# Norm products issued later, key normalisation moved to the last projection pairs, the gate's loops exchanged, and a second bank for the filler, in a hybrid attention and state-space block

## The chip, the cores and the metric

The kernel runs on one core of one Trainium2 chip. The metric is the time of one execution of the program on the device, in microseconds; a comparison goes by the median of several runs. A core has one matrix engine (PE, whose weight loads are listed apart as PEld), three engines for elementwise work (DVE, ACT and POOL), and an engine, SP, that in this kernel issues all the DMA transfers between the main memory and the on-chip buffers (SBUF). Matrix products land in PSUM, which is divided into banks of 128 x 512 single-precision numbers.

## The reference

One decoder layer in single precision, sequence 1024, width 2048. In one row per operation:

```
h = rms_norm(x) * gain
q, k, v, z_att, u, z_ssm, g_att, g_ssm = split(h @ w_in)            # widths 6 x 1024, 2 x 2048
q, k = rms_norm over each group of 64 channels, with gains           # 8 heads x 2 halves
w  = softmax(q0 k0^T / 8, causal) - lam * softmax(q1 k1^T / 8, causal)
y_att = rms_norm(w @ v, per head) * (1 - lam_init) * silu(z_att)
y  = gelu(diagonal state-space scan of u + d * u)
y_ssm = y * sigmoid(y @ w_glu + b_glu) * silu(z_ssm)
m  = sigmoid(g_att) * (y_att @ w_proj_att) + sigmoid(g_ssm) * (y_ssm @ w_proj_ssm)
out = x + m @ w_out
```

## The kernel before

Every large product keeps single-precision accuracy by splitting both operands into a high and a low part (`split`, lines 90 and 91: ACT rounds to the high part, DVE or POOL subtracts for the low one), and by three matrix products, high by high, high by low, low by high. A matrix instruction here multiplies a 128 x 128 block of weights by 128 x 512 activations. Everything is kept channels-first (128 channels on the partitions, 512 tokens along the row); a value called t is one of the two halves of the 1024 tokens.

The program has these stages in the order of time:

- **Projections.** The products with `w_in` are computed by a scheme of the Strassen-Winograd kind: a *pair* of output tiles (256 channels by 1024 tokens) over half of the 2048 input channels costs 7 block products of 12 matrix instructions (`products`, line 492), and additions on the results in place of an eighth product (`pair`). The first half of the input channels goes through `part`, which stores its results to `d_p`; the second half goes through `whole`, which loads them again (tag `q`, pool `qp`, line 555) and adds them (lines 571 to 582). Between is the state-space scan, whose result y lies in main memory as `d_yg`. The pairs of `whole` come in the order q (4 pairs, i = 0 to 3), k (4 to 7), v (8 to 11), z_att ("za", 12 to 15), z_ssm ("zs", 16 to 19), g_att ("ga", 20 to 27) and g_ssm ("gs", 28 to 35). The last two products of a pair (`rest`) are put off into the next pair by `pending` and `finish`.
- Each finished tile of `whole` goes through a function of its kind. `evac_q` and `evac_k` store it and call `norms`: ACT squares the tile, it is split (tiles `sh_`, two buffers, and `sl_`, one buffer, the same tags in which q, k and v are split for their stores), and two matrix products with a selector (line 975, into the banks `nps`) add up the squares of each group of 64 channels. `qk_norms` turns the 32 rows of sums into inverse roots; its three steps are called behind pairs n = 8, 10 and 12, that is, in the v pairs and the first za pair. `norms_k` has 16 tiles of k to normalise: load from `d_k` (line 1004, tag `ks`, one buffer), load the factors (`rb`, line 1007), multiply on DVE (line 1015), split, store. One step is called behind each pair from i = 12 on; the last ones where they fall. `evac_gate` computes silu(z) for za and zs (sigmoid on ACT, line 1034, product on POOL, line 1035) and the sigmoid for ga and gs (line 1037), and stores.
- **Gate** (`w_glu`): for each token half t and each of 8 column tiles ct, 24 matrix instructions (line 1135), the weights loaded (line 1121) and split anew for either half; y (line 1127) and silu(z_ssm) (line 1129) are loaded and multiplied on POOL (line 1130), times the sigmoid of the product on DVE (line 1138), split, stored to `d_ys` (line 1142).
- **Attention**, 8 heads of 8 query tiles, in the order `ORDER`. The matrix engine's order is written by hand here: scores (line 1178), mask (line 1181), DVE scales and takes the row's bound (line 1185), ACT exponentiates (line 1187), later PE transposes (line 1203) and multiplies by v (line 1215, bank `op`) and sums squares (line 1232, same bank). Between them *filler* instructions are fed, of which `FILL` gives the number behind each query tile: the products y_ssm @ `w_proj_ssm` (`ps_tile`, line 288). Each filler tile is 24 instructions into one bank (`ac2`), which DVE then multiplies by the gate g_ssm (line 292).
- **Tail**: what is left of the filler, the products with `w_proj_att`, and the products with `w_out` (line 1356).

Outside the attention the order on each engine is made by a list scheduler that simulates the program. The order is fixed in the program: each engine works its list in turn and waits at semaphores. SP's transfers are in one such list too.

Of the kernel before, what the change touches and what calls it, by code (L numbers as in the profile page):

```python
# [10 lines left out]
F32 = mybir.dt.float32  # L11
# [24 lines left out]
FILL = (10, 9, 10, 9, 10, 9, 10, 9)  # L36
# [31 lines left out]
def hybrid_block(ctx: ExitStack, tc: tile.TileContext, x_t, x_n, w_t, w_v, w_glu, w_pa, w_ps,  # L68
# [257 lines left out]
    with ExitStack() as pa_ctx:  # L326
# [158 lines left out]

        def products(ps, i, a, w, start):
            hs, ls = a
# [7 lines left out]
        pending = []  # L495
# [6 lines left out]
        def pair(w, a, out11, out21, out22, out12):  # L502
# [19 lines left out]
            u3 = post.tile([P, 512], F32, name="u3", tag="u3")  # L522
# [422 lines left out]
        qp = ev_ctx.enter_context(tc.tile_pool(name="qp", bufs=8, side="right"))  # L945
# [7 lines left out]
        def qk_norms():  # L953

            for t in range(2):
                v = stg.tile([32, 512], F32, name="nv", tag="sq")
                y = stg.tile([32, 512], F32, name="ny", tag="ny", bufs=1)
# [10 lines left out]
        def norms(src, row, t):  # L968

            sq = stg.tile([P, 512], F32, name="sq", tag="sq")  # L970
            A.activation(sq, src, AF.Square)
            hi, lo = split_tiles()
            split(hi, lo, sq)
            for n, m in enumerate((hi, lo)):
                T.matmul(nps[t], lhsT=sel[:, 32 - row:160 - row], rhs=m,
                         start=(n_norms[t] == 0), stop=(n_norms[t] == 31), skip_group_check=True)
                n_norms[t] += 1
# [63 lines left out]
        evacs = {"q": evac_q, "k": evac_k, "v": evac_v, "za": evac_gate(d_za, True), "zs": evac_gate(d_zs, True),  # L1041
                 "ga": evac_gate(d_ga, False), "gs": evac_gate(d_gs, False)}
        first = {kind: i for kind, i, _ in KINDS}
        for i, (kind, n) in enumerate(order):
# [3 lines left out]
            if n == 8:  # L1048
                steps = qk_norms()
            if n in (8, 10, 12):  # L1050
                next(steps, None)
            if i == 12:
                ks = norms_k()
            if i >= 12:
                next(ks, None)
        finish()
        ev_ctx.close()
# [39 lines left out]
        gl = gl_ctx.enter_context(tc.tile_pool(name="gl", bufs=3))  # L1097
# [7 lines left out]
        def yg_inputs(t):  # L1105
            def ld(k, hi, lo):
                r = wp.tile([P, 512], F32, name="ya", tag="value", bufs=2)
                D.dma_start(r, d_yg[k, :, t * 512:(t + 1) * 512])
                split(hi, lo, r)
            return ld  # L1110

        for t in range(2):
            tk = slice(t * 512, (t + 1) * 512)
            ya = act_half(act, yg_inputs(t))
            for ct in range(8):
                for _ in range(2 if 8 * t + ct > 2 else 0):
                    next(head0, None)
                ws = []
                for b in range(2):
                    raw = wp.tile([P, 4, P], F32, name="w_raw", tag="w_raw", bufs=5)  # L1120
                    D.dma_start(raw, w_glu[ct, :, 4 * b:4 * b + 4])
                    m = (2 * ct + b) % 7
                    hi, lo = (wp.tile([P, 4, P], F32R, name=n, tag=f"{n}{m}") for n in ("w_hi", "w_lo"))
                    split(hi, lo, raw)
                    ws.append((hi, lo))
                r = gl.tile([P, 512], F32, name="r", tag="r")
                D.dma_start(r, d_yg[ct, :, tk])
                z = gl.tile([P, 512], F32, name="z", tag="z")
                D.dma_start(z, d_zs[ct, :, tk])
                Q.tensor_tensor(r, r, z, ALU.mult)  # L1130
                ps = acc.tile([P, 512], F32, name="pg", tag="acc")
                for k in range(8):
                    wh, wl = (x[:, k % 4] for x in ws[k // 4])
                    for n, (x, y) in enumerate(((wh, ya[0][k]), (wh, ya[1][k]), (wl, ya[0][k]))):
                        T.matmul(ps, lhsT=x, rhs=y, start=(k == 0 and n == 0), stop=(k == 7 and n == 2))
                sg = gl.tile([P, 512], F32, name="sg", tag="sg", bufs=2)
# [303 lines left out]
```

## Time and profile before

| what | value |
|---|---|
| time before, median of 3 runs (lowest, highest) | 2805.34 us (2804.27, 2805.68) |
| the profiled execution's own time | 2804.28 us |
| its span in the profile | 2802.5 us |
| PE busy | 2695.5 us, 96%, 12402 matrix instructions |
| DVE, ACT, POOL busy | 66%, 43%, 27% |
| DMA moved | 487.82 MB, mean 174 GB/s |

A row of the profile names an engine, an operation with its output and its inputs, a line of the kernel, and times; "<-" behind an idle time names what ended it. A window gives, between two times from the span's start, the busy time of each engine with the number of its instructions in brackets, then the clock granted to PE as a share of full speed (PEclk), the share of the time in which the DMA engines were busy, and GB/s. A row of the waits gives an engine and line, what it waited for, the microseconds in total, how often, and the longest one. In a timeline, the columns are the start, the duration, the engine and line, the operation, and in square brackets the idle time of that engine before it. SPq, ACTq and the like are the engines' own sequences of issued transfers and semaphore waits.

### The profile page before, as it was taken

The page shows a single profiled execution, that of the slowest core. Times are in us where ns is not written, and L with a number is a line of the kernel's source. Part 1 is how long each engine was busy: PE and PEld are TensorE (multiplying, and loading weights), DVE is VectorE, ACT ScalarE, POOL GpSimd, SP SyncE. Part 2 cuts the span into 40 slices and gives each one's busy share as a digit, 9 for nine tenths or more (in the row PEclk, how much of TensorE's full clock was granted, in tenths as well). Part 3 has the DMA queues.
Part 4 walks back from the last instruction along what each step waited for, and adds up shares of the span by engine and source line. Part 5 has one row for each costly group of instructions (what it writes and reads, how often), then busy time and mean ns, then how long its engine had stood idle before and what let it go on. Part 6 is the DMA issues. An engine that isn't in the chain of part 4 may idle for free. (4 is left out here: it accounts for less than half of the span.)

```text
span 2802.5 us, 37947 instructions
## 1 busy us (share of the span) xinstructions
PE 2695.5 (96%) x12402; PEld 2205.5 (79%) x12402; DVE 1844.1 (66%) x3512; ACT 1205.9 (43%) x2359; POOL 743.7 (27%) x1101
## 2 busy tenths in 40 slices
PE   9999999999999998998899999789999999999999
PEld 8888788887878876776678888667878778888887
DVE  4998877777787776787676666457666575325432
ACT  6433455545455544433444444345555433223221
POOL 0002866565674011224442222212222200000000
PEclk9999999999999999999999999999999999999999
DMA  9653333333333454457765555976777386455453
GB/s 350 220 180 115 103 113 117 115 116 120 121 101 117 166 181 165 149 174 230 243 214 167 168 162 169 317 234 194 198 238 206 128 296 194 131 155 177 150 158 113
DMA packets 261926, 487.82 MB, mean 174 GB/s; under 512 B 33912, under 2 KB 44480, under 8 KB 261728
## 3 DMA queue, kind: packets, MB, share of 16 engines
q1 hardware_dynamic: 261728, 485.40, 53.7%
q8 instruction: 98, 1.61, 0.2%
q14 instruction: 100, 0.82, 0.1%
HBM read 345.72 MB, written 139.56 MB: 173 GB/s over the span
## 5 line engine op out<-in xcount | busy, mean ns | idle before, releaser
L492 PE MATMUL acc<-ah,w_hi 128*128 128x512 f32 x2128 | 841.6, 396 | 28.1 <-ACT u L523 22.8
L492 PE MATMUL acc<-ah,w_lo 128*128 128x512 f32 x2128 | 841.0, 396 | 0.0
L492 PE MATMUL acc<-al,w_hi 128*128 128x512 f32 x2128 | 840.2, 395 | 0.0
L90 ACT ACTIVATE w_hi<-w_raw 128x512 fp32r<-128x512 f32 x532 | 333.9, 629 | 523.3 <-PE o L1356 219.7
L91 DVE TENSOR_TENSOR w_lo<-w_raw,w_hi 128x512 fp32r<-128x512 f32 x474 | 338.4, 715 | 308.9 <-ACT w_hi L90 296.3
L492 PEld LDWEIGHTS acc<-ah,w_hi 128*128 128x128 f32 x2128 | 402.7, 189 | 120.6 <-ACT u L523 27.6
L492 PEld LDWEIGHTS acc<-ah,w_lo 128*128 128x128 f32 x2128 | 402.5, 189 | 87.7 <-issue 5.4
L492 PEld LDWEIGHTS acc<-al,w_hi 128*128 128x128 f32 x2128 | 402.9, 189 | 83.4 <-issue 2.0
L90 ACT ACTIVATE w_hi<-value 128x512 fp32r<-128x512 f32 x304 | 191.7, 630 | 313.3 <-DVE value L346 161.4
L91 DVE TENSOR_TENSOR w_lo<-value,w_hi 128x512 fp32r<-128x512 f32 x304 | 219.5, 722 | 61.3 <-ACT w_hi L90 53.7
L1356 PE MATMUL o<-w_lo,mh 128*128 128x512 f32 x512 | 199.2, 389 | 0.0
L1356 PE MATMUL o<-w_hi,ml 128*128 128x512 f32 x512 | 199.2, 389 | 0.0
L1356 PE MATMUL o<-w_hi,mh 128*128 128x512 f32 x512 | 195.3, 389 | 0.0
L581 POOL TENSOR_TENSOR u<-u,q 128x512 f32<-128x512 f32 x72 | 99.8, 1387 | 230.2 <-ACT u L514 120.7
L346 DVE TENSOR_TENSOR value<-w_raw 128x512 f32<-128x512 f32 x152 | 150.3, 989 | 2.7
L1185 DVE TENSOR_SCALAR_CACHE_REDUCE pe<-s,nrq 128x128 f32<-128x128 f32 (+7 forms) x128 | 100.1, 813 | 70.9 <-PE s L1181 58.9
L91 POOL TENSOR_TENSOR w_lo<-w_raw,w_hi 128x512 fp32r<-128x512 f32 x58 | 84.0, 1448 | 234.3 <-ACT w_hi L90 204.0
L575 POOL TENSOR_TENSOR p<-p,q 128x512 f32<-128x512 f32 x36 | 60.5, 1680 | 322.5 <-DVE acc L520 210.0
L288 PE MATMUL pc<-ah,w_hi 128*128 128x512 f32 x256 | 107.6, 420 | 25.4 <-DVE z L292 16.8
L1187 ACT ACTIVATE pe<-pe,mx 128x128 f32<-128x128 f32 (+7 forms) x128 | 98.5, 773 | 42.2 <-DVE pe L1185 42.0
L1356 PEld LDWEIGHTS o<-w_lo,mh 128*128 128x128 f32 x512 | 96.1, 188 | 20.0
L1356 PEld LDWEIGHTS o<-w_hi,mh 128*128 128x128 f32 x512 | 96.1, 188 | 19.9
(681 smaller groups left out, 4588.5 us busy)
## 6 DMA issues: line engine op xcount, KB each, us to landing
w_raw<-in_w_t_dram SPq DMA_DIRECT2D x288, 256.0 KB
q<-d_p SPq DMA_DIRECT2D x160, 256.0 KB
w_raw<-in_w_out_dram SPq DMA_DIRECT2D x128, 256.0 KB
d_p<-u SPq DMA_DIRECT2D x72, 256.0 KB
w_raw<-in_w_ps_dram SPq DMA_DIRECT2D x64, 256.0 KB
w_raw<-in_w_pa_dram SPq DMA_DIRECT2D x64, 256.0 KB
d_p<-ps SPq DMA_DIRECT2D x52, 256.0 KB
d_p<-p SPq DMA_DIRECT2D x36, 256.0 KB
```

What stands on the lines that cost most here:

```text
L90: A.activation(hi, src, AF.Copy)
L91: (eng or V).tensor_tensor(lo, src, hi.bitcast(F32), ALU.subtract)
L288: T.matmul(ps, lhsT=w[:, k % 4], rhs=b[k], start=(k == 0 and n == 0), stop=(k == 7 and n == 2))
L346: V.tensor_tensor(t, x, y, ALU.add)
L492: T.matmul(ps, lhsT=x[:, c], rhs=y[i][j], start=(start and j == 0 and n == 0), stop=(j == 3 and n == 2), skip_group_check=True)
L575: e.tensor_tensor(u, u, other(1), ALU.add)
L581: e.tensor_tensor(u, u, other(i), ALU.subtract)
L1185: V.tensor_scalar(pc[c][:, 0:w], sc[c][:, 0:w], nrq[:, 2 * h + c, tt:tt + 1], None, ALU.mult, ALU.min, accum_out=mx[:, c:c + 1])
L1187: ins = A.activation(pc[c][:, 0:w], pc[c][:, 0:w], AF.Exp, bias=mx[:, c:c + 1], scale=-1.0, accum_out=su[:, c:c + 1])
L1356: T.matmul(ps[i], lhsT=a[k][:, tt], rhs=w[:, 0], start=(k == 0 and n == 0), stop=(k == KT - 1 and n == 2))
```

## The change

1. `norms`: the two selector products are put on a list and issued when three more block products have begun (`postponed`, `tick`), and its split has tiles of its own (`nh`, `nl`, two buffers each). To make room, `qp` has 5 buffers in place of 8.
2. The PSUM copy `u3` of a pair alternates between two tiles in the pairs of `whole`.
3. The three steps of `qk_norms` come one pair later, and `norms_k` starts at i = 20 (the first ga pair) in place of i = 12 (the first za pair).
4. The zs tiles are multiplied by y as well as by the sigmoid: each of the 16 tiles loads y from `d_yg` (tag `ks`, one buffer) and has a DVE product more. The gate no longer loads y for this, and has no product on POOL.
5. The gate has the column tile in the outer loop, the token half in the inner one: each weight block is loaded and split once. Both halves of y are therefore held at once, the second in tiles of `kq`. The first column tile's weights and the first half of y are issued ahead of the last products of the projections.
6. In the attention the pool `wtp` is opened before `pex`, so the tiles of the exponentials lie elsewhere in SBUF.
7. The filler alternates between its bank and the bank `op` of the values, where no values or sums of squares are due; `give_bank` finishes a filler tile that holds `op` before these come. `FILL` feeds 74 instructions a head in place of 76.

```diff
-FILL = (10, 9, 10, 9, 10, 9, 10, 9)
+FILL = (10, 9, 9, 9, 10, 9, 9, 9)
...
+        tick, postponed = [0], []
+
         def products(ps, i, a, w, start):
+            tick[0] += 1
+            while postponed and postponed[0][0] <= tick[0]:
+                postponed.pop(0)[1]()
...
-            u3 = post.tile([P, 512], F32, name="u3", tag="u3")
+            turn[0] ^= 1
+            if more and turn[0]:
+                u3 = more[0].tile([P, 512], F32, name="u3", tag="u3", bufs=1)
+            else:
+                u3 = post.tile([P, 512], F32, name="u3", tag="u3")
...
-        qp = ev_ctx.enter_context(tc.tile_pool(name="qp", bufs=8, side="right"))
+        more.append(stg)
+        qp = ev_ctx.enter_context(tc.tile_pool(name="qp", bufs=5, side="right"))
...
-            hi, lo = split_tiles()
+            hi, lo = (stg.tile([P, 512], F32R, name=n, tag=n) for n in ("nh", "nl"))
             split(hi, lo, sq)
-            for n, m in enumerate((hi, lo)):
-                T.matmul(nps[t], lhsT=sel[:, 32 - row:160 - row], rhs=m,
...
+            def add():
+                for m in (hi, lo):
+                    T.matmul(nps[t], lhsT=sel[:, 32 - row:160 - row], rhs=m,
...
+            postponed.append((tick[0] + 3, add))
...
-        def evac_gate(dst, silu):
+        def evac_gate(dst, silu, src=None):
...
+                    if src is not None:
+                        y = stg.tile([P, 512], F32, name="y", tag="ks", bufs=1)
+                        D.dma_start(y, src[i, :, t * 512:(t + 1) * 512])
+                        V.tensor_tensor(st, st, y, ALU.mult)
                     Q.tensor_tensor(st, st, sg, ALU.mult)
...
-            if n == 8:
+            if n == 9:
                 steps = qk_norms()
-            if n in (8, 10, 12):
+            if n in (9, 11, 13):
                 next(steps, None)
-            if i == 12:
+            if i == 20:
                 ks = norms_k()
-            if i >= 12:
+            if i >= 20:
                 next(ks, None)
...
+        ahead = gate_weights(0)
+        ya = act_half(act, yg_inputs(0, lambda: wp.tile([P, 512], F32, name="ya", tag="value", bufs=2)))
         finish()
+        run(ks)
...
-        for t in range(2):
-            tk = slice(t * 512, (t + 1) * 512)
-            ya = act_half(act, yg_inputs(t))
-            for ct in range(8):
-                for _ in range(2 if 8 * t + ct > 2 else 0):
+        for ct in range(8):
+            ws, ahead = ahead, gate_weights(ct + 1) if ct < 7 else None
+            for t in range(2):
+                tk = slice(t * 512, (t + 1) * 512)
+                if 2 * ct + t > 1:
                     next(head0, None)
...
-                r = gl.tile([P, 512], F32, name="r", tag="r")
-                D.dma_start(r, d_yg[ct, :, tk])
-                z = gl.tile([P, 512], F32, name="z", tag="z")
-                D.dma_start(z, d_zs[ct, :, tk])
-                Q.tensor_tensor(r, r, z, ALU.mult)
+                r = gl.tile([P, 512], F32, name="r", tag="r", bufs=3)
+                D.dma_start(r, d_zs[ct, :, tk])
...
+        wtp = at.enter_context(tc.tile_pool(name="wtp", bufs=1))
         pex = at.enter_context(tc.tile_pool(name="pex", bufs=2))
-        wtp = at.enter_context(tc.tile_pool(name="wtp", bufs=1))
...
+        def filler_bank():
+            turn[0] ^= 1
+            if ended:
+                return bank(ssp, "s")() if turn[0] else bank(ac2)()
+            own[0] = bool(turn[0]) and (at_step[0] < NT - 2 or not 0.2 < at_step[0] % NT < 4.3)
+            return bank(tps, "op")() if own[0] else bank(ac2)()
...
+        def give_bank():
+
+            while own[0]:
+                owed[0] -= 1
+                step()
```

Three places show how the instructions move. The first is PE in the q pairs, where `acc<-` rows are block products and `nps` rows the selector products of the norms. Before:

```order
L975 MATMUL nps_11009<-sl__11252,sel 128x512
L975 MATMUL nps_11009<-sh__11278,sel 128x512
L975 MATMUL nps_11009<-sl__11279,sel 128x512
L975 MATMUL nps_11010<-sh__11322,sel 128x512
L492 MATMUL acc<-ah,w_hi 128x512
L492 MATMUL acc<-al,w_hi 128x512
```

and after:

```order
L497 MATMUL acc<-ah,w_lo 128x512
L987 MATMUL nps_11009<-nl,sel 128x512
L497 MATMUL acc<-ah,w_hi 128x512
L497 MATMUL acc<-al,w_hi 128x512
L497 MATMUL acc<-ah,w_lo 128x512
L497 MATMUL acc<-ah,w_hi 128x512
L987 MATMUL nps_11009<-nh,sel 128x512
L497 MATMUL acc<-al,w_hi 128x512
```

Four selector products stood in a row, each on another tile; now each stands alone among block products.

The second place is DVE in the projections: the product of k with its factors (L1015, then L1028), the product with y (L1051), and the additions that empty the banks (L571, L582, L520; then L580, L591, L525). Before, in the za pairs:

```order
L1015 TENSOR_TENSOR ks<-ks,rb 128x512
L91 TENSOR_TENSOR w_lo<-w_raw,w_hi 128x512
L366 TENSOR_TENSOR value<-value,w_raw 128x512
L571 TENSOR_TENSOR q<-acc,q 128x512
L91 TENSOR_TENSOR sl__15302<-ks,sh__15301 128x512
```

After, in the zs pairs and then in the ga pairs:

```order
L1051 TENSOR_TENSOR p_14095<-p_14095,y 128x512
L591 TENSOR_TENSOR u_14110<-acc,u_14110 128x512
L91 TENSOR_TENSOR w_lo<-value,w_hi 128x512
L91 TENSOR_TENSOR w_lo<-w_raw,w_hi 128x512
L366 TENSOR_TENSOR value<-value,w_raw 128x512
L1051 TENSOR_TENSOR u_14110<-u_14110,y 128x512
L580 TENSOR_TENSOR q<-acc,q 128x512
L91 TENSOR_TENSOR w_lo<-w_raw,w_hi 128x512
L1051 TENSOR_TENSOR q<-q,y 128x512
...
L591 TENSOR_TENSOR u_15246<-acc,u_15246 128x512
L1028 TENSOR_TENSOR ks<-ks,rb 128x512
L91 TENSOR_TENSOR w_lo<-w_raw,w_hi 128x512
L91 TENSOR_TENSOR sl__16114<-ks,sh__16113 128x512
L585 TENSOR_TENSOR p_15156<-acc,p_15156 128x512
L91 TENSOR_TENSOR w_lo<-value,w_hi 128x512
L346 TENSOR_TENSOR value<-value,w_raw 128x512
L1028 TENSOR_TENSOR ks<-ks,rb 128x512
```

The normalisation of k has gone from the za and zs pairs to the ga and gs pairs, with a step every six to ten instructions of DVE in both; the zs pairs have four products with y each, in DVE's order right before or behind the additions that empty the banks.

The third place is DVE where the gate ends and the attention starts, with what each instruction waits for (DMAHW0 to DMAHW7 are counters of landed transfers). Before:

```order
L91 TENSOR_TENSOR yl<-r,yh 128x512 [waits DMAHW4_49,Activation_49]
L1138 TENSOR_TENSOR r<-r,sg 128x512 [waits Activation_49,Pool_49]
L91 TENSOR_TENSOR yl<-r,yh 128x512 [waits DMAHW7_49,Activation_49]
L1185 TENSOR_SCALAR pe,mx<-s,nrq 128x640 [waits DMAHW3_49,DMAHW4_49,DMAHW2_49,DMAHW5_49,DMAHW1_49,DMAHW6_49,DMAHW0_49,DMAHW7_49,DVE_49,PE_49]
L1185 TENSOR_SCALAR pe,mx<-s,nrq 128x640 [waits PE_49]
```

and after:

```order
L1165 TENSOR_TENSOR r<-r,sg 128x512 [waits DMAHW5_49,Activation_49]
L1212 TENSOR_SCALAR pe,mx<-s,nrq 128x640 [waits PE_49]
L91 TENSOR_TENSOR yl<-r,yh 128x512 [waits DMAHW4_49,Activation_49]
L1212 TENSOR_SCALAR pe,mx<-s,nrq 128x640 [waits PE_49]
L1218 RECIPROCAL sums<-su 128x2 [waits Activation_49]
```

The first scaling of scores waited for transfers of all eight counters and for PE; it now waits for PE alone and stands ahead of the gate's last split.

More of the change, by code (lines that the diff above doesn't have):

```diff
@@ L493, in products @@
                              stop=(j == 3 and n == 2), skip_group_check=True)
-        pending = []
+        pending, turn, more = [], [0], []
         def finish():
@@ L1047, in hybrid_block, with yg_inputs, ld, gate_weights @@
             w = None
-            if n == 8:
+            if n == 9:
                 steps = qk_norms()
-            if n in (8, 10, 12):
+            if n in (9, 11, 13):
                 next(steps, None)
-            if i == 12:
+            if i == 20:
                 ks = norms_k()
-            if i >= 12:
+            if i >= 20:
                 next(ks, None)
+        def yg_inputs(t, raw):
+            def ld(k, hi, lo):
+                r = raw()
+                D.dma_start(r, d_yg[k, :, t * 512:(t + 1) * 512])
+                split(hi, lo, r)
+            return ld
+        def gate_weights(ct):
+            ws = []
+            for b in range(2):
+                raw = wp.tile([P, 4, P], F32, name="w_raw", tag="w_raw", bufs=5)
+                D.dma_start(raw, w_glu[ct, :, 4 * b:4 * b + 4])
+                m = (2 * ct + b) % 6
+                hi, lo = (wp.tile([P, 4, P], F32R, name=n, tag=f"{n}{m}") for n in ("w_hi", "w_lo"))
+                split(hi, lo, raw)
+                ws.append((hi, lo))
+            return ws
+        ahead = gate_weights(0)
+        ya = act_half(act, yg_inputs(0, lambda: wp.tile([P, 512], F32, name="ya", tag="value", bufs=2)))
         finish()
+        run(ks)
         ev_ctx.close()
@@ L1103, in hybrid_block @@
         head0 = first_head()
[L1105 to L1110, printed above, removed]
[L1112 to L1130 removed]
+        pairs = [kq.tile([P, 2, 512], F32R, name="y2", tag=x) for x in
+                 ("qs0", "kh0", "kl0", "qs1", "kh1", "kl1", "vh", "vl")]
+        ya = [ya, ([x[:, 0] for x in pairs], [x[:, 1] for x in pairs])]
+        load = yg_inputs(1, lambda: gl.tile([P, 512], F32, name="ya", tag="ya", bufs=4))
+        for k in range(8):
+            load(k, ya[1][0][k], ya[1][1][k])
+        for ct in range(8):
[3 more added lines that the diff above has]
+                if 2 * ct + t > 1:
+                    next(head0, None)
+                r = gl.tile([P, 512], F32, name="r", tag="r", bufs=3)
+                D.dma_start(r, d_zs[ct, :, tk])
                 ps = acc.tile([P, 512], F32, name="pg", tag="acc")
@@ L1262, in feed, with step @@
                 owed[0] -= 1
-                if next(fill, 0):
+                if step():
                     return
+        def step():
+            done = next(fill, 0)
+            if done:
+                own[0] = False
+            return done
+        def give_bank():
+            while own[0]:
+                owed[0] -= 1
+                step()
         with tc.manual_schedule(engines={T.engine}):
@@ L1285, in hybrid_block @@
                     drain(i + 0.9)
+            give_bank()
             ended.append(1)
```

30 lines of the change are left out of this document (17 added, 13 removed).

## The prediction

> **What bounds the kernel now.** I read the page's head first, then a table of windows cut at the stages, and looked for waits only in the windows where the matrix engine loses time.
>
> ```profile
> span 2802.5 us, 37947 instructions
> PE 2695.5 (96%) x12402; PEld 2205.5 (79%) x12402; DVE 1844.1 (66%) x3512; ACT 1205.9 (43%) x2359; POOL 743.7 (27%) x1101
> ```
>
> PE is busy 96% of the span, so a gain lies in its gaps or in fewer matrix instructions. The change removes none that matter. The windows (length, then PE, PEld, DVE, ACT and POOL busy with counts, PE's clock, DMA share, GB/s) are: q pairs, two stretches of k pairs, v, za, zs, the first ten ga and gs pairs, gate, start of attention, attention, last products.
>
> ```profile
> core 0: us, PE busy (x) PEld busy (x) DVE busy (x) ACT busy (x) POOL busy (x), PEclk, DMA share, GB/s
> 1001.41:1116.70 115.29, 98.97 (x391) 78.02 (x391) 75.01 (x103) 52.51 (x90) 18.80 (x13) 0.91 0.48 162
> 1116.70:1176.64 59.94, 58.80 (x255) 47.54 (x255) 42.11 (x59) 30.07 (x53) 11.76 (x9) 1.00 0.47 154
> 1176.64:1270.36 93.72, 91.53 (x432) 74.55 (x431) 76.73 (x119) 36.24 (x64) 20.50 (x13) 1.00 0.52 176
> 1270.36:1368.89 98.53, 84.94 (x349) 66.56 (x348) 69.27 (x93) 37.65 (x67) 43.54 (x28) 0.95 0.73 234
> 1368.89:1452.27 83.38, 76.28 (x325) 61.13 (x324) 63.70 (x78) 34.78 (x63) 40.09 (x28) 0.98 0.72 235
> 1452.27:1641.04 188.77, 188.77 (x834) 156.33 (x833) 122.89 (x161) 83.65 (x140) 42.69 (x30) 1.00 0.52 168
> 1752.40:1858.20 105.80, 89.89 (x364) 69.44 (x362) 51.96 (x65) 39.65 (x68) 28.32 (x19) 0.94 0.89 288
> 1858.20:1873.36 15.16, 5.21 (x20) 3.06 (x20) 2.33 (x5) 1.32 (x2) 0.00 (x0) 0.80 0.95 328
> 1873.36:2214.58 341.22, 315.95 (x1729) 271.21 (x1730) 239.15 (x573) 184.96 (x427) 90.64 (x64) 0.97 0.69 195
> 2292.64:2797.00 504.36, 504.36 (x2225) 417.62 (x2226) 202.74 (x311) 136.08 (x217) 0.00 (x0) 1.00 0.51 158
> ```
>
> The ga and gs row is PE at its pace: no gap, full clock, 188.77 / 834 = 0.2263 us an instruction, 84 x 0.2263 = 19.0 us a pair. I price each other stage as length minus count x 0.2263; this takes in the slower clock that the gaps bring. Lost are: q 115.29 - 88.5 = **26.8**, k 2.2 in the stretch shown, v 93.72 - 91.53 = 2.2 of plain gaps (its transposes are short, so the count does not serve), za 98.53 - 79.0 = **19.5**, zs 83.38 - 73.5 = **9.8**, gate 105.80 - 82.4 = **23.4**, the start 15.16 - 4.5 = **10.6**. In attention instructions have many sizes; there 341.22 - 315.95 = 25 are plain gaps.
>
> **The change, part by part.**
>
> *Norms behind (q).* In q, PE waits for the low part of the squares:
>
> ```profile
> PE nps L975 <- DVE sl__11279 L91: 3.5, 1, 3.5
> PE nps L975 <- DVE sl__11487 L91: 3.4, 1, 3.4
> PE nps L975 <- DVE sl__11695 L91: 3.5, 1, 3.5
> DVE sl__11323 L91 <- DMA d_q<-sl__11315: 2.2, 1, 2.2
> 1041.06 0.32 SPq L981 DMA_DIRECT2D d_q<-sl__11315  x1
> 1043.20 0.97 DVE L91 TENSOR_TENSOR sl__11323<-sq,sh__11322 128x512 fp32r<-128x512 f32 x1 [2.17 <-DMA d_q<-sl__11315]
> ```
>
> The one `sl_` buffer passes from the store of q's low half to the norm's split: DVE waits until the store issued at 1041.06 has landed at 1043.20, 2.15 us, and holds the additions that empty the banks behind it. With `nl` of its own that wait goes, and three products of slack (36 x 0.2263 = 8.1 us) cover ACT's square and split. The store-to-store chain through `sl_` stays: two DVE instructions of about 0.97 at most and the landing, under 4.1 us, four times a pair are 16.4 of 19.0 us, so it fits. Left over, as in k (2.2 us over 3 pairs), a little: 3.8. Gain **-23**; bounds -18 (a third of the gaps has another cause) and -26.8 (all). k and v: 0.
>
> *Normalisation of k.* In za the chain is this:
>
> ```profile
> DVE ks L1015 <- DMA ks<-d_k: 23.0, 10, 6.1
> 1300.37 0.63 ACT L90 ACTIVATE sh__14061<-ks 128x512 fp32r<-128x512 f32 x1 [3.35 <-DVE ks L1015]
> 1300.90 0.58 ACT L523 ACTIVATE u<-acc 128x512 f32<-128x512 f32 x1
> 1301.53 0.50 PE L492 MATMUL acc<-ah,w_hi 128*128 128x512 f32 x1 [2.62 <-ACT u L523]
> 1290.37 0.69 DVE L1015 TENSOR_TENSOR ks<-ks,rb 128x512 f32<-128x512 f32 x1 [2.23 <-DMA rb<-d_rk]
> 1339.15 0.69 DVE L1015 TENSOR_TENSOR ks<-ks,rb 128x512 f32<-128x512 f32 x1 [6.06 <-DMA ks<-d_k]
> 1342.63 0.53 SPq L1004 DMA_DIRECT2D ks<-d_k  x1
> 1346.70 1.81 DVE L1015 TENSOR_TENSOR ks<-ks,rb 128x512 f32<-128x512 f32 x1 [0.23 <-DMA ks<-d_k]
> 1423.88 0.69 DVE L1015 TENSOR_TENSOR ks<-ks,rb 128x512 f32<-128x512 f32 x1 [1.15 <-DMA d_zs<-q]
> ```
>
> DVE waits for the load of k into its one buffer; ACT, in order, stands at the split of it (3.35 us); behind that ACT's copy of the bank (line 523) is late, and PE waits 2.62 for the bank. ACT's turn is what is late, not the copy's tile, so two u3 tiles are worth 0. Fourteen steps from 1290.37 to 1423.88 take 9.54 us each; the shortest, 1339.15 to 1346.70, 7.55, with the load landing in 4.07.
>
> The change takes these steps out of za: **-18.5** (19.5 less 1 left; bounds -16 and -19.5). It does not end them: they run in the ga and gs pairs, which lose nothing now, at the order's same rate of 15 steps over 5.8 pairs. PE gives a step 19.0 x 5.8 / 15 = 7.4 us. If a step takes 9.54 there, ga and gs lose 15 x (9.54 - 7.4) = +32; at 7.55, +2. The same loads, stores and one buffer come together there as in za, whose DMA share was 0.73 beside 0.52 in ga, so I take a mean step of 9.0: **+24**, nearer to the upper end.
>
> The Trainium skill ("DMA: Bandwidth & Descriptors", section "Latency and other measured facts") says that access to main memory, the largest part of a transfer's fixed 2 us, rises with load, and that a lighter load makes the fixed cost smaller. The trace agrees: 2.15 us landing at share 0.48, 4.07 at 0.73. By that, were the ga pairs to stay at their 0.52, the step would be near the short end and the total near rival A's.
>
> *y in zs.* With the k steps gone, zs would lose nothing; it gets four DVE products a pair, each after a load that can only be issued when the product before has freed the tile. A cycle is 0.69 (product) + 0.53 (issue) + 2.15 to 4.6 landing (4.07 seen, and one issue more ahead of it) = 3.4 to 5.8 us; four are 13.5 to 23.3 of 19.0 us a pair. So the loss over four pairs lies between 0 and 4 x 4.3 = 17; I take 8, since the addition that empties a bank stands right behind a waiting product. Against 9.8 now: **-2** (bounds -9.8 and +7). ACT's sigmoids and POOL's products remain. `qp` with 5 buffers: the q loads must lead by one pair, 19 us, against 4 us landing, so 0.
>
> *Gate.*
>
> ```profile
> PE pg L1135 <- ACT w_hi L90: 11.2, 4, 9.8
> PE pg L1135 <- ACT ah L90: 4.7, 3, 3.3
> 1800.00:1810.00 10.00, 5.80 (x14) 3.77 (x15) 9.35 (x9) 6.64 (x13) 6.86 (x4) 0.54 1.02 364
> w_raw<-in_w_glu_dram SPq DMA_DIRECT2D x32, 256.0 KB
> r<-d_yg SPq DMA_DIRECT2D x16, 256.0 KB
> ```
>
> In the ten microseconds where the second half begins, DMA is full (1.02) and the clock falls to 0.54. PE waits 11.2 for weights and 4.7 for the halves of y. The change takes away 16 of the 32 weight loads and the 16 loads of y: 32 x 0.25 MB = 8 MB, at 288 GB/s 29 us of transfers in a stage of 106; the y loads, though, now run in zs, costed above. The weights' split halves too (16 x 0.63 on ACT). The two waits of 15.9 go, and part of the slow clock. What is late next are the stores to `d_ys`, as many as before. I take 7 lost in place of 23.4, **-16** (bounds -10 and -21).
>
> *Start of attention.*
>
> ```profile
> 1865.78 0.81 SPq L1142 DMA_DIRECT2D d_ys<-yl  x1
> 1872.42 0.89 DVE L1185 TENSOR_SCALAR_CACHE_REDUCE pe<-s,nrq 128x640 f32<-128x640 f32 x1 [11.33 <-DMA oz<-d_za]
> 1873.36 0.47 PE L1178 MATMUL s<-kh,qs 128*128 128x128 f32 x1 [7.76 <-DVE pe L1185]
> ```
>
> The first scaling lies in the memory of the gate's tiles and waits until the last `d_ys` store, issued at 1865.78, is through: DVE 11.33 idle, PE 7.76. In the new order that instruction waits for PE alone, and stands ahead of the last split. Left are 2.6 of the 10.6 (the last gate tile's sigmoid and stores, on which the filler's input waits): **-8** (bounds -4 and -10.6).
>
> *Second bank.*
>
> ```profile
> PE pc L288 <- DVE z L292: 10.9, 6, 3.0
> PE pc L288 <- DVE sums L1191: 5.4, 2, 2.7
> ```
>
> Both are a filler tile's first instruction that finds its one bank not yet emptied, 16.3 together. With every second tile in `op` those at tiles that get it go, and the tile behind them finds `ac2` long empty. But `op` is barred for over half of a head's time in the second half of its steps, and `give_bank` may push some filler ahead of the values, so that less is left to cover the transposes. I take 6 left: **-10** (bounds -14 and 0). The 16 filler instructions less are done later, 16 x 0.2263 = 3.6 us in attention and 3.6 again in the tail: 0.
>
> By the Trainium skill ("TensorE: Matmul & The Clock Gate", section "HAM oscillation — how this bites in real kernels"), "Adding PSUM double-buffering gave no further gain" in its kernel, where DMA set the pace. No run here shows it; by it this term is 0 and the total is rival C's.
>
> **Sum**: -23 - 18.5 + 24 - 2 - 16 - 8 - 10 = **-53.5**, with 0 for u3, `qp` and `FILL`. From the profiled execution's own 2804.28 (its span and 1.8 around it): 2750.8. The median of the runs stands 1.06 above that execution, so **2752 us**.
>
> **The rivals.**
>
> A. *The stall does not come back.* Landing in ga is 2 us as in q; the step then fits, ga loses 2 and zs none. For it: ga's share is 0.52, q's stores landed in 2.15. Against: za had these loads and much the same others. -53.5 - 22 - 8 = -83.5: 2722.
>
> B. *It comes back whole.* ga +32 in place of +24, and zs's four cycles 5.8 each, 17 lost in place of 8: +17, so 2769. For it: the traffic of za (0.73) was k's own, and it goes along.
>
> C. *The second bank brings nothing*, as the waits are really DVE's turn: the second row names the reciprocal at line 1191 and not the multiply at 292. +10: 2762.
>
> D. *Slower: the y tile as a DVE block.* If a y cycle takes as long as a k step, 9.54 us (its load queued on SP behind stores that wait for POOL, the next product behind it), four are 38.2 in a pair of 19.0: zs loses 76.5 in place of 8, +68.5, so 2820. The gain is gone from a cycle of 8.6 us on (61 us over four pairs). Against: y is loaded from an array done long before, and is neither split nor stored under that tag.
>
> **How the numbers follow.** The forecast, 0.40; A 0.20, B 0.18, C 0.10, D 0.07; nothing moves (a second stall elsewhere takes about what is won) 0.05. The forecast's own range is 2738 to 2766, from the bounds of the single terms, not added up. The range from just under A to the middle between B and no change, **2718 to 2788**, leaves out D, the last case and a little beside A and B. A change of under 0.2%, 5.6 us, could not be told from none. Faster takes in forecast, A, B and C: 0.88; slower D: 0.07; within 0.2%: 0.05.
>
> **What would show it.** q: no `nps` row over 1 us, window near 92 us. za: about 80. ga and gs: the product with `rb` waits for `ks` for several us and PE for the u3 copies, clock under 1.00; if clock is 1.00, A. zs: waits of DVE line 1051 for y; under 8 us in total means nothing lost. Gate: about 89 us, no wait for `w_hi` over 2. Start: no 7.76. Filler: both bank rows under 3. I am wrong if ga and gs lose over 40, if zs is longer than now, or if what q gains is lost in k.

## The result and the profile after

The changed kernel takes 2740.56 us (median of 4 runs, 2738.02 to 2741.47) beside 2804.81 us of the kernel before: a ratio of 0.977, with a 95% interval of 0.9753 to 0.9787. The forecast was 2752 us, in a range of 2718 to 2788. The profiled execution's span fell from 2802.5 to 2739.7 us. Medians and ratios leave out executions in a slower state of the chip, of which e4 below had one (2854 us).

The page's head of the changed kernel, and its windows cut at the same additions as in the table of before ("q", from the second q pair to the first k pair, "k", the other three k pairs, v, za, zs, the eight ga pairs, six gs pairs), then the gate from its first product and the start of the attention:

```profile
span 2739.7 us, 37819 instructions
PE 2675.3 (98%) x12402; PEld 2197.7 (80%) x12402; DVE 1845.8 (67%) x3512; ACT 1195.8 (44%) x2343; POOL 715.7 (26%) x1085
...
core 0: us, PE busy (x) PEld busy (x) DVE busy (x) ACT busy (x) POOL busy (x), PEclk, DMA share, GB/s
1002.26:1091.58 89.32, 87.38 (x377) 69.61 (x376) 76.13 (x105) 53.56 (x95) 19.46 (x13) 1.00 0.65 210
1091.58:1154.62 63.04, 63.04 (x278) 51.79 (x276) 45.09 (x62) 32.78 (x55) 12.79 (x9) 1.00 0.48 151
1154.62:1239.22 84.60, 84.60 (x402) 69.83 (x401) 68.61 (x104) 31.19 (x55) 21.43 (x12) 1.00 0.57 187
1239.22:1318.42 79.20, 78.62 (x352) 64.56 (x351) 68.71 (x84) 33.60 (x59) 42.15 (x28) 1.00 0.54 175
1318.42:1399.66 81.24, 79.30 (x349) 64.96 (x348) 71.26 (x82) 32.00 (x56) 37.83 (x27) 1.00 0.62 202
1399.66:1579.43 179.77, 158.99 (x659) 126.85 (x658) 117.94 (x161) 72.48 (x128) 36.24 (x25) 0.96 0.71 234
1579.43:1693.67 114.24, 114.24 (x505) 94.64 (x504) 73.64 (x97) 50.47 (x85) 25.51 (x18) 1.00 0.52 166
1729.54:1817.65 88.11, 84.61 (x364) 69.03 (x362) 33.73 (x50) 31.61 (x53) 3.84 (x3) 0.98 0.88 266
1817.65:1836.00 18.35, 16.88 (x90) 14.30 (x91) 13.63 (x35) 10.28 (x24) 4.17 (x3) 1.00 0.92 276
```

In the projections PE is at full clock and loses 2 us or less to gaps in every stage but one: the eight ga pairs take 179.77 us, where before they took 150.7, and their clock is 0.96. What was lost in za is lost here. The gate still has 3.5 us of gaps, at a clock of 0.98. The same cuts made in every run give the table below, in us of the profiled executions. "Gate" is from the last but one gs pair's addition to the first scores, "attention" from there to the first product with `w_out`; the six gs pairs are 114.2 in every run, and what stands before q and behind the attention is the same within 4 us. In the changed kernel and the runs without an edit in the attention, that stage takes 480.8 to 487.5 us, but for the 492.2 of e8; a few us there tell nothing by themselves.

| run | q | k | v | za | zs | ga | gate | attention | span |
|---|---|---|---|---|---|---|---|---|---|
| before | 115.3 | 59.9 | 93.7 | 98.5 | 83.4 | 150.7 | 141.8 | 504.5 | 2802.5 |
| changed | 89.3 | 63.0 | 84.6 | 79.2 | 81.2 | 179.8 | 124.0 | 483.0 | 2739.7 |
| e1 norms as before | 104.3 | 59.3 | 94.2 | 80.0 | 80.9 | 180.9 | 123.3 | 484.3 | 2763.1 |
| e5 own tiles, products at once | 88.7 | 63.0 | 84.6 | 79.2 | 82.5 | 178.9 | 122.8 | 483.8 | 2738.4 |
| e6 products later, shared tiles | 103.3 | 58.2 | 94.4 | 80.0 | 81.4 | 178.7 | 123.2 | 486.1 | 2761.7 |
| e2 k from za on | 90.1 | 63.0 | 84.7 | 88.5 | 97.0 | 163.2 | 121.2 | 480.8 | 2743.7 |
| e3 k paced | 89.0 | 63.0 | 84.6 | 79.2 | 82.1 | 149.0 | 127.8 | 484.1 | 2713.5 |
| e11 k paced, early | 88.5 | 63.0 | 84.6 | 79.2 | 82.2 | 150.9 | 122.3 | 487.5 | 2715.4 |
| e8 y in the gate | 89.0 | 63.0 | 84.7 | 99.7 | 89.2 | 149.6 | 122.2 | 492.2 | 2744.5 |
| e9 weights twice | 88.4 | 63.0 | 84.6 | 79.2 | 81.8 | 177.6 | 124.0 | 484.7 | 2739.6 |
| e12 halves outside | 89.2 | 63.0 | 84.6 | 79.2 | 81.3 | 180.2 | 132.8 | 485.0 | 2748.4 |
| e7 exponentials' tiles back | 90.6 | 63.0 | 84.6 | 79.2 | 82.8 | 179.0 | 122.7 | 490.6 | 2748.8 |
| e4 one bank | 88.6 | 63.0 | 84.6 | 79.2 | 83.0 | 176.4 | 124.1 | 494.7 | 2750.0 |
| e10 one u3 | 88.7 | 63.0 | 84.7 | 79.2 | 82.4 | 181.7 | 123.2 | 484.6 | 2741.7 |

The waits that answer to those quoted of before: in the q stretch (1002 to 1091 us) all of PE's; in the ga pairs (1399 to 1580) PE's for the copies u3, DVE's for the factors and the tiles of k, and ACT behind it; in zs (1318 to 1400) DVE's for y and PE's; then the summary of DVE's products of k with their factors (shortest, median, longest in ns, first and last start), and PE's first scores and waits for the filler's bank.

```profile
PE nps L987 <- DVE nl L91: 1.4, 3, 0.9
PE acc L497 <- DVE u L591: 0.5, 1, 0.5
...
PE acc L497 <- ACT u L532: 15.8, 6, 4.6
DVE ks L1028 <- DMA rb<-d_rk: 15.7, 3, 5.7
DVE ks L1028 <- DMA ks<-d_k: 13.4, 8, 3.4
ACT sh__15769 L90 <- DVE ks L1028: 5.9, 1, 5.9
...
DVE q L1051 <- DMA y<-d_yg: 3.9, 3, 2.1
PE acc L497 <- ACT u L532: 1.9, 2, 1.0
...
L1028 DVE TENSOR_TENSOR ks<-ks,rb x16: 692/693/1677, 1403.0 to 1543.6; 128x512 f32<-128x512 f32 x16
...
1817.65 0.50 PE L1205 MATMUL s<-kh,qs 128*128 128x512 f32 x1 [0.84 <-ACT sg L1164]
...
PE pc L288 <- ACT w_hi L90: 5.9, 1, 5.9
PE pc L288 <- DVE z L292: 5.3, 3, 3.1
```

The 3.5 us waits at the selector products are gone (longest 0.9). The chain DVE for a load, ACT for DVE, PE for ACT's copy stands in ga as it stood in za. The first scores run through. In the bank's place a 5.9 us wait for the split of a filler weight has appeared.

### The profile page after: what moved, and what is told of

Its sections match the earlier page's. It is cut to its first block, busy times and chain, and to the rows that moved or that the text cites. A ratio compares the mean times of both kernels' runs of the same rounds, so it can differ in the third digit from the quotient of the medians.

```text
span 2739.7 us, 37819 instructions
## 1 busy us (share of the span) xinstructions
PE 2675.3 (98%) x12402; PEld 2197.7 (80%) x12402; DVE 1845.8 (67%) x3512; ACT 1195.8 (44%) x2343; POOL 715.7 (26%) x1085
## 5 line engine op out<-in xcount | busy, mean ns | idle before, releaser
L497 PE MATMUL acc<-ah,w_hi 128*128 128x512 f32 x2128 | 839.7, 395 | 24.5 <-ACT u L532 19.0
L90 ACT ACTIVATE w_hi<-w_raw 128x512 fp32r<-128x512 f32 x516 | 323.9, 629 | 527.7 <-PE o L1409 240.1
L91 DVE TENSOR_TENSOR w_lo<-w_raw,w_hi 128x512 fp32r<-128x512 f32 x458 | 324.1, 708 | 288.1 <-ACT w_hi L90 279.5
L91 DVE TENSOR_TENSOR w_lo<-value,w_hi 128x512 fp32r<-128x512 f32 x304 | 229.4, 755 | 60.3 <-ACT w_hi L90 52.6
L346 DVE TENSOR_TENSOR value<-w_raw 128x512 f32<-128x512 f32 x152 | 160.5, 1056 | 2.8
L1409 PEld LDWEIGHTS o<-w_hi,ml 128*128 128x128 f32 x512 | 96.1, 188 | 19.9
```

The lines of the kernel that those rows point to most:

```text
L90: A.activation(hi, src, AF.Copy)
L91: (eng or V).tensor_tensor(lo, src, hi.bitcast(F32), ALU.subtract)
L346: V.tensor_tensor(t, x, y, ALU.add)
L497: T.matmul(ps, lhsT=x[:, c], rhs=y[i][j], start=(start and j == 0 and n == 0), stop=(j == 3 and n == 2), skip_group_check=True)
L1409: T.matmul(ps[i], lhsT=a[k][:, tt], rhs=w[:, 0], start=(k == 0 and n == 0), stop=(k == KT - 1 and n == 2))
```

## The experiments

All are one edit on the changed kernel, of which the main lines are shown ("..." marks what is left out). Ratios are to the kernel before, measured on the same chip. From chip to chip the median of the kernel before lies between 2802.57 and 2805.53 us, so 3 us between two runs can be the chip.

**The norms.** Three runs take apart what part 1 does: e1 has both pieces of this edit, e5 the second alone, e6 the first alone.

```diff
-            hi, lo = (stg.tile([P, 512], F32R, name=n, tag=n) for n in ("nh", "nl"))
+            hi, lo = split_tiles()
...
-            postponed.append((tick[0] + 3, add))
+            add()
```

> The changed kernel with one part undone: the norms' split again in the tiles that q, k and v share, and the two selector products issued at once. Theory (the shared low tile, held until its store has landed, held DVE and so PE): the q window grows from 89 to about 112 us, with PE waits of 3 us and more at the selector products, and the total is 2741 + 23 = 2764 us. Rival (the q pairs gained from the other edits of this stage, two u3 or fewer q buffers): the total stays within 5 us of 2741.

> The changed kernel with the norms' split in tiles of its own, but the two selector products issued at once and not three block products later. Theory (the wait for the store of the shared low tile was the cause): nearly all of the gain stays, 2741 to 2746 us. Rival (the later products were the cause): 2760 us or more.

> The changed kernel with the selector products three block products later, but the norms' split in the shared tiles again. Theory (DVE is held by the shared low tile, whatever PE does): most of the 25 us that both undone cost comes back, 2755 to 2766 us. Rival (PE no longer waits, so the held DVE is covered): 2741 to 2748 us.

Measured: e1 2765.74 us (0.9862, 0.9841 to 0.9882), e5 2743.79 (0.9791, 0.9777 to 0.9806), e6 2764.46 (0.9863, 0.9849 to 0.9878). All that the norms gained hangs on the tiles of their own; issuing the products later brought nothing that can be told (0.9770 beside 0.9791, intervals that overlap). The q window of e1 and of e6, and what PE waits for there (990 to 1130 us) in e6:

```profile
1002.64:1106.90 104.26, 96.18 (x393) 74.52 (x392) 76.68 (x103) 50.88 (x88) 18.62 (x13) 0.97 0.53 175
...
1002.92:1106.20 103.28, 95.43 (x393) 73.71 (x393) 76.39 (x103) 51.44 (x90) 18.84 (x13) 0.98 0.55 179
PE acc L497 <- ACT p L515: 5.4, 3, 1.9
```

With the products late, PE no longer stands at them, but at banks that ACT copies late: the held engine is what costs, wherever PE meets it. The expectation of e1 was wrong in its detail: the q window grew to 104 and not to 112, with no wait of 3 us at the selector products, and most of the rest of the 23 us came in k and v (59.3 + 94.2 beside 63.0 + 84.6, 5.9 more).

What holds DVE at the shared low tile shows in its idle time ahead of writing it. In e1's q window, ahead of the norms' splits (line 91), DVE stands 6.5 us in all until stores of q's low half have landed. Ahead of q's own splits (line 1004) it stands 9.0 us in all until the selector products have read the norms' low half. The longest of either kind:

```profile
DVE sl__11115 L91 <- DMA d_q<-sl__11107: 2.4, 1, 2.4
...
DVE sl__11479 L1004 <- PE nps L987: 2.3, 1, 2.3
```

In e6 the two sums are 7.9 and 8.2 us, in the kernel before 14.2 and 8.2. In the changed kernel the wait for the products is gone and the norms' splits wait for no store, but q's own splits still wait 5.8 us for the stores ahead of them, which PE does not feel. So it was the one low tile passing to and fro between stores and products, and not the stores alone. The new tiles are also two of each kind; whether a second buffer of the shared tiles would have done as much was not run.

**Where k is normalised.** In e2:

```diff
-            if i == 20:
+            if i == 12:
                 ks = norms_k()
-            if i >= 20:
+            if i >= 12:
                 next(ks, None)
```

> The changed kernel with the normalisation of k started at the first za pair again; y and k now share one buffer in the zs pairs. Theory (a step costs some 2 us of PE wherever it runs faster than its load lands): za and zs lose again some 20 to 30 us, ga loses 10 to 15 in place of 29, and the total is 2735 to 2755 us. Rival (the move itself was the gain, ga being the cheaper place): 2760 us or more. Rival (ga was the worse place): 2720 us or less.

Measured: 2750.07 us (0.9817, 0.9794 to 0.984). za and zs lose 9.3 and 15.8, ga gains 16.6, all as the theory had it. So the move is worth some 9 us (8.5 in these three windows, 4.0 in the whole span of the profiled executions), and that while y and k share one buffer in zs. What it is worth without y comes from e8, which was made for another question.

```diff
-        evacs = {... "zs": evac_gate(d_zs, True, d_yg),
+        evacs = {... "zs": evac_gate(d_zs, True),
...
-                D.dma_start(r, d_zs[ct, :, tk])
+                D.dma_start(r, d_yg[ct, :, tk])
+                z = gl.tile([P, 512], F32, name="z", tag="z")
+                D.dma_start(z, d_zs[ct, :, tk])
+                Q.tensor_tensor(r, r, z, ALU.mult)
```

> The changed kernel with y loaded and multiplied in the gate again (on POOL) and not in the zs pairs; the gate's loops and its single weight loads stay. Theory (the y loads cost the zs pairs about 2 us; in the gate they are 4 MB more on DMA engines that are 0.88 busy, 15 us of transfers against 10 us of room): zs gains 2, the gate loses 5 to 15, total 2744 to 2754 us. Rival (the gate has room for them, the weights alone were too much): 2738 to 2742 us.

Measured: 2750.01 us (0.9814, 0.9799 to 0.9828), within the expectation, but not by its way. The products of k with their factors, in e8:

```profile
L1028 DVE TENSOR_TENSOR ks<-ks,rb x16: 679/692/1512, 1276.2 to 1416.7; 128x512 f32<-128x512 f32 x16
```

They run from 1276.2 on, in the za pairs, though the program starts them at the first ga pair. In e2, where the program starts them at the first za pair, they begin at the same place (1276.0). So the program's place did not set theirs; what had held the steps back in the changed kernel was y, which has the same buffer all through zs. With it gone they went forward from the ga pairs into za and zs. So e8 is no clean trial of y. It is one of the place: za, zs and ga together are 338.5 us with the steps in za and zs, and 340.2 with y in zs and the steps in ga. The move by itself gains next to nothing: the steps cost PE some 29 us in either place. Of e8's own edit it can be said that the gate took the second load and the POOL product without growing (122.2 us), and that the attention behind it grew by 9.2. In its first 33 us PE there waits 6.3 us for the filler's inputs, which are loads from `d_ys` (1.5 in the changed kernel), so the loads put back may be paid for behind the gate; the rest of the 9.2 has no cause shown.

**Pacing the steps.** In e3 every product of k stands behind the addition that empties its pair's first bank:

```diff
-                V.tensor_tensor(st, st, rb, ALU.mult)
+                ins = V.tensor_tensor(st, st, rb, ALU.mult)
+                after(ins, added[-1])
...
-                V.tensor_tensor(q, ps, q, ALU.add)
+                added.append(V.tensor_tensor(q, ps, q, ALU.add))
```

> The changed kernel with one added order on DVE: each product of k with its factors comes behind the addition that empties the first bank of its pair, so one step a pair over all ga and gs pairs in place of two to three a pair; its load then has a pair's 19 us to land. Theory (DVE waits for the load in its one buffer, ACT behind it, PE behind ACT): the 29 us lost in the ga pairs go but for 1 or 2 us, PE's clock there is 1.00, total 2713 us. Rival (the steps' own work on DVE, ACT and the queue is what crowds the pairs, not the wait): the loss is spread over 16 pairs and the total is 2730 us or more.

Measured: 2716.06 us (0.9688, 0.9668 to 0.9708), 24.5 us under the changed kernel (by the two ratios 0.9916 of it); no other run but e11 comes near it. The windows of e3 for the eight ga pairs and six gs pairs, and PE's longest wait behind them:

```profile
1399.33:1548.32 148.99, 148.99 (x659) 123.41 (x658) 103.24 (x144) 71.67 (x119) 36.48 (x25) 1.00 0.67 222
1548.32:1662.56 114.24, 114.24 (x505) 94.63 (x504) 77.03 (x109) 54.89 (x91) 26.48 (x18) 1.00 0.67 221
...
PE pg L1163 <- issue: 7.4, 1, 7.4
```

The same 16 steps, loads, splits and stores now cost PE nothing: the stretch is as long as PE is busy, at full clock, with DMA at 0.67. It was the wait and not the work. Of the 30.8 us gained in ga, 3.8 are lost again in the gate, where PE stands 7.4 us in the first column tiles: the last steps now run beside the gate's first loads. In e11 there are two steps in each of the pairs 20 to 23. The product stands behind the last addition that the pair makes itself, or, for the second step, behind the first of the two that are put off into the next pair:

```diff
-                V.tensor_tensor(u, ps, u, ALU.add)
+                added.append(V.tensor_tensor(u, ps, u, ALU.add))
                 done(*at[1], u)
+                if hooks:
+                    hooks.pop()()
...
+                    if i == 2:
+                        added.append(ins)
...
                 next(ks, None)
+                if i < 24:
+                    hooks.append(lambda: next(ks, None))
```

> The changed kernel with the normalisation of k ordered as in the paced run, but with two steps in each of the first four ga pairs, so that it ends four pairs ahead of the gate. Theory (the paced run's last steps, beside the gate's first loads, cost the 7.4 us that PE stands in the gate's first columns there): ga loses nothing, that wait goes, total 2707 to 2711 us. Rival (two steps in a pair of 19 us are too many, at 7.6 to 9.5 us each): ga loses 2 to 8 us and the total is that of the paced run, 2716, or more.

Measured: 2717.6 us (0.9686, 0.9673 to 0.9699): no better than e3. The wait went, as the theory said (gate 122.3 beside 127.8), but 1.9 came back in ga and 3.4 in the attention, so the total is the rival's. PE's waits there, from 1790 us on, in e11 and then in e3:

```profile
PE pc L288 <- ACT w_hi L90: 7.3, 1, 7.3
PE s L1212 <- DMA kh<-d_k: 5.2, 3, 3.2
...
PE pc L288 <- ACT w_hi L90: 8.5, 1, 8.5
PE s L1206 <- DMA kh<-d_k: 3.4, 3, 1.6
```

The scores of a head wait 1.8 us longer for its keys. The rest of the 3.4 I have not traced; it is less than the attention differs between runs that do not touch it. That the wait goes when the steps end earlier is shown; that this saves time is not.

**The gate.** In e9 each weight block is loaded and split for either half:

```diff
-                D.dma_start(raw, w_glu[ct, :, 4 * b:4 * b + 4])
+                D.dma_start(raw, w_glu[ct // 2, :, 4 * b:4 * b + 4])
...
-            ws, ahead = ahead, gate_weights(ct + 1) if ct < 7 else None
             for t in range(2):
+                ws, ahead = ahead, gate_weights(2 * ct + t + 1) if 2 * ct + t < 15 else None
```

In e12 the token half is outside, its y goes into the tiles of the first half, and each weight block is loaded and split for either half as in e9:

```diff
...
+        for t in range(2):
+            if t:
+                ya = act_half(act, yg_inputs(1, ...))
+            for ct in range(8):
+                ws, ahead = ahead, gate_weights(8 * t + ct + 1) if 8 * t + ct < 15 else None
```

> The changed kernel with the gate's weights loaded and split once for each token half again (32 loads in place of 16), in the new loop order. Theory (half of the gate's gain is traffic and splits): 4 MB more against DMA engines 0.88 busy, the gate 5 to 15 us longer, total 2746 to 2756 us. Rival (what counted was the work put ahead of the last products and the end of the load burst in the middle): 2740 to 2744 us.

> The changed kernel with the token half in the gate's outer loop again: the second half of y is loaded and split into the tiles of the first when these are read, and each weight block is loaded and split twice. The first weights and the first half of y stay ahead of the last products, and the gate still loads only silu(z) y. Loading the weights twice alone cost nothing (run of the weights twice). Theory (the exchange gained by ending the burst of loads and splits in the middle, where DMA was full and the clock fell): PE waits again for the halves of y and for weights in the middle, gate 8 to 14 us longer, total 2749 to 2755 us. Rival (the gain came from what is put ahead of the last products, and from one product and one load less a tile): total within 4 us of 2741.

Measured: e9 2743.74 us (0.9781, 0.9767 to 0.9794), e12 2747.57 (0.9802, 0.9784 to 0.982). Loading and splitting every weight block twice costs nothing in the new order: the gate is 124.0 us in e9 as in the changed kernel. With the halves outside it is 8.8 us longer, within what was expected, and mostly in one place (the total, 7 us longer, came out a little under the expectation). PE's waits in e12's gate, and the longest of them in the timeline:

```profile
PE pg L1158 <- ACT ah L90: 9.2, 4, 5.9
...
1772.56 1.22 PE L1158 MATMUL pg<-ah,w_hi 128*128 128x512 f32 x2 [5.89 <-ACT ah L90]
```

At 1772 us the second half of y is to be loaded and split into the tiles that the last products have just read. That is half of the 17.8 us of the gate. The other half may lie in what is put ahead of the last products and in the load and product less a tile; e8 says of the latter that the gate alone does not mind them. What was put ahead was not taken back in a run, so the cause of this half stays open.

**The start of the attention and the second bank.** In e7 and in e4:

```diff
-        wtp = at.enter_context(tc.tile_pool(name="wtp", bufs=1))
         pex = at.enter_context(tc.tile_pool(name="pex", bufs=2))
+        wtp = at.enter_context(tc.tile_pool(name="wtp", bufs=1))
```

```diff
-            own[0] = bool(turn[0]) and (...)
+            own[0] = False and (...)
```

> The changed kernel with the exponentials' pool opened ahead of the other one again, so that the tiles lie where the gate's tiles lay. Theory: the first scaling waits for the gate's last stores again, PE stands some 8 us at the start of the attention, total 2747 to 2750 us. Rival (the last gate column is bound by something else, the filler's inputs above all): 2741 to 2744 us.

> The changed kernel with the filler in its one bank all through the attention. Theory: the waits of the filler's first products for DVE come back, 10 to 15 us, total 2751 to 2756 us. Rival (DVE's turn is what is waited for, and a second bank brings nothing): 2741 to 2744 us.

Measured: e7 2748.62 us (0.9804, 0.9785 to 0.9824), e4 2751.82 (0.9817, 0.9798 to 0.9837). The interval of e7 just meets that of the changed kernel (0.9753 to 0.9787), that of e4 does not. The attention is 7.6 and 11.7 us longer; together 19.3 of the 21.5 that came off it from before to changed. They lie above the 480.8 to 487.5 us of most runs that do not touch it, but e7 by little, so the waits have to say what came back. PE's waits from 1690 to 2250 us, in e7 and then in e4:

```profile
PE pc L288 <- DVE z L292: 11.5, 4, 6.3
PE s L1205 <- DVE pe L1212: 5.6, 1, 5.6
...
PE pc L288 <- DVE z L292: 13.9, 9, 3.2
PE pc L288 <- ACT w_hi L90: 8.6, 2, 7.4
```

The wait of the first scores is back in e7 (5.6 us; the kernel before had 7.76), and one of 6.3 at the filler's bank, more than the 5.3 in all of the changed kernel. In e4 the bank's waits are 13.9 + 1.6 for the sums beside 5.3.

**The second u3.** In e10:

```diff
-            if more and turn[0]:
+            if False:
```

> The changed kernel with one tile for the PSUM copy u3 again. Theory (the copy's tile was never what was waited for): 2739 to 2743 us, no difference. Rival (the ga pairs, where PE waits for these copies 16 us, need the second tile): 2746 us or more.

Measured: 2743.2 us (0.9777, 0.9764 to 0.979) beside 0.977: no difference that can be told.

## Why the prediction was right, point by point

The forecast was -53.5 us on the profiled execution; its span fell by 62.8. The windows alone mislead here: in the changed kernel 24 instructions more fall into the zs window (349 for 325), and 21 fewer into q, k and v. So the table gives beside the windows what each stage lost by the prediction's own pricing (length less count x 0.2263, plain gaps for v), before and after.

| term | forecast | windows, before to changed | by that pricing | its own run |
|---|---|---|---|---|
| norms (q, k, v) | -23 | -32.0 | 31.2 to 4.1: -27.1 | e1: +23.4 |
| k out of za | -18.5 | -19.3 | 19.5 to -0.5: -20.0 | |
| y in zs | -2 | -2.1 | 9.8 to 2.3: -7.5 | |
| k into ga and gs | +24 | +29.1 | 0 to 30.6: +30.6 | e3: -30.8 |
| gate | -16 | -17.8 | 23.4 to 5.7: -17.7 | e12: +8.8, e9: 0 |
| start of attention | -8 | -21.5 with the bank | | e7: +7.6 |
| second bank | -10 | | | e4: +11.7 |
| two u3 | 0 | | | e10: 0 |

The way of the change and the main step, that the loss in za goes along into ga, are as forecast. That the total came within 12 us is in part luck, since the misses work against one another: ga and gs lost 6.6 us more than forecast, while zs gained 5.5 more and the norms 4.1 more.

- **Norms.** That the shared low tile is the cause holds, and the q window's loss is 89.32 - 377 x 0.2263 = 4.0, forecast 3.8. Two things were missing. The tile is held by the selector products as well as by the store: DVE stands 9.0 us for them in e1, 6.5 for stores. And the size was met in part by luck: undoing part 1 puts 11.3 us back in the q window (15.3 lost in e1), 5.3 in k and v, and 4.5 in za, where I had put nothing. Another 11.5 us in q (26.8 before, 15.3 in e1) came from an edit that I had priced at nothing; DVE's waits for stores there fell from 14.2 to 6.5 us with it. It may be the second u3 while the norms are the old ones, the fewer q tiles, or the inverse roots one pair later; e10 tells only that u3 is worth nothing with the new norms. Which it is stays open. Too much was said for the three products of slack: e5 has none and lost nothing that can be told.
- **k.** The step was right that the loss goes along, and nearly right in its size: 16 products from 1403.0 to 1543.6 are 9.37 us a step, where I took 9.0; 15 x (9.37 - 7.4) = 30 against the 30.6 measured. Rival A, with steps at 7.55, is excluded, rival B (+32) was near for this term. What I had not seen is why the steps come where they do: not by the pair in which the program starts them but by the buffer that y holds (e8).
- **The lighter load.** The Trainium skill ("DMA: Bandwidth & Descriptors", section "Latency and other measured facts") would have led to rival A if ga had kept its DMA share. It did not: the share rose to 0.71 with the steps, beside 0.73 in za before. So the row, taken with its own conditions, was the better guide; against the rule itself nothing speaks, though the two landings that I had set beside it are a store's (2.15) and a load's (4.07). e3 shows that even at 0.67 no loss need follow.
- **y in zs.** DVE waited 3.9 us in all for y, and zs lost 2.3 where I took 8. That the window's -2.1 agrees with the forecast's -2 is chance: the 24 instructions more make up the difference from -7.5. So the addition behind a waiting product, for which I took 8, cost little.
- **Gate.** The sum was right and its reason half wrong. I had put the gain down first to 8 MB less on full DMA engines. e9 puts back 4 MB and 16 splits of weights at no cost; e8 puts back the other 4 MB without making the gate longer, but with a longer attention behind it. What is shown to count is the burst in the middle, the second half of y into tiles in use: 8.8 us (e12). The other 9 stay open.
- **Start and bank.** Both near the forecast, -7.6 for -8 and -11.7 for -10, each read from the attention of one profiled execution. The row that I had quoted for the start names a load, `oz<-d_za`, as the last to land, and not the `d_ys` store; e7 shows that the place of the tiles is the cause, not which transfer ended the wait. The waits bear the two terms out: 5.6 us at the first scores in e7, 13.9 + 1.6 at the bank in e4 beside 5.3. Rival C falls: in this kernel the second bank gained what the Trainium skill's sentence on PSUM double-buffering ("TensorE: Matmul & The Clock Gate", section "HAM oscillation — how this bites in real kernels") did not find in its own; what limited that kernel once it had been rewritten the page does not say. Left over by the bank rows is 5.3, where I had said under 3, with a new wait of 5.9 for a filler weight.
- **Rival D** falls: a y cycle never took what a k step takes; PE waited 1.9 us in all in the zs pairs.

## What to carry to other kernels

When a load, a product and a split in one buffer are moved from stages that suffer to stages that have slack, ask what sets their rate: a scheduler that runs them as fast as its model says they can go runs them too fast in the new place as well, and e3 got from one added order on DVE, one step a pair, over a third as much again as the whole change had gained. A single tile that passes between two results, one read by a store and one by the matrix engine, holds an engine that works in order at both, and its later work is late too: here 23 us, ended by tiles of their own for one of the two. And before a gain is put down to bytes, put the bytes back: loading the gate's weights twice cost nothing. Last, count the instructions in two windows before their lengths are compared.

## What the runs showed that I had not expected

- The place in the program did not set the place in time: in e8 the 16 steps, written from the first ga pair on, all ran ahead of it, since their buffer was free (products from 1276.2 to 1416.7 us; the first ga addition, by the table's cuts, at 1427).
- DMA share and loss do not go together: 0.67 with no loss (e3), 0.71 with 30 us lost (changed), at the same transfers.
- The two orders that paced k differ by 5.5 us in the gate and agree in the total within their intervals, since the attention took 3.4 of it back and ga 1.9.
